# Gate pre-activations of two branches as seven block products ahead of attention, their tanh parked in memory until the merges

## The chip, the cores and the metric

One core of a Trainium2 chip runs the whole kernel; the other cores do nothing. The metric is the device time of one execution in microseconds (us), lower is better. The engines of the core are TensorE (PE in the profile; its weight loads are PEld), VectorE (DVE), ScalarE (ACT), GpSimd (POOL) and SyncE (SP), which issues nearly all DMA transfers. Each engine works its own instruction stream in order, and semaphores connect the streams.

## What is computed

An encoder of two post-norm layers on 512 tokens of width 1024, in float32. One input projection of 6816 columns feeds three mixers and the gates; the part that matters here:

```python
proj = jnp.einsum('bsd,de->bse', x, w_in[l])
(na_q, na_k, na_v, df_q, df_k, df_v, m_cq, m_ckv, m_kr, gate_pre) = jnp.split(proj, split_points, axis=-1)
na_out = neighbourhood_attention(...)     # branch 0, 8 heads of 64
df_out = diff_attention(...)              # branch 1, 4 heads of 2 x 64
mla_out = latent_attention(...)           # branch 2, 8 heads
gates = jax.nn.sigmoid(gate_pre + b_gate[l]).reshape(b, s, 3, 1024)
merged = sum(gates[:, :, i] * (branch_i @ w_branch[l, i]) for i in range(3))
x = layer_norm(alpha * x + merged @ w_out[l], ln1)
gu = x @ w_ffn_in[l]                      # 2 x 2816 columns
x = layer_norm(alpha * x + (silu(gu[..., :2816]) * gu[..., 2816:]) @ w_ffn_out[l], ln2)
```

The gates need only x, not the attention: 3 x 1024 columns for 512 tokens. The kernel uses sigmoid(z) = (1 + tanh(z/2))/2, with the half taken later.

## The kernel before

Every float32 operand is split into a high part and a low rest (`split`, `wsplit`: ScalarE writes the high part, VectorE subtracts it, which gives the low one), and a product is three matmuls, high by high, high by low and low by high (`mm3`). x stands transposed in `xth` and `xtl` (eight blocks of 128 rows, 512 tokens). Weights come by DMA in blocks of 512 KB into a ring of two tiles `raw`, are split into `whi` and `wlo`, and are used by `gemm_w` (weights stationary) or `gemm_x` (activations stationary). PSUM has two banks each under the names `acc`, `sc`, `pv` and `tr`. SBUF slots are handed out by two queues: H with 8 tiles `f` of 1024 columns, R with 38 tiles `r` of 512.

A layer runs: neighbourhood values (`na_values`), the latent input projection with its norms (`latents`), four pairs of neighbourhood heads (`na_pair`), four pairs of latent heads (`mla_proj`, `mla_pair`), four differential heads (`df_proj`, `df_values`, `df_head`), the output projection, and the feed-forward part. In the feed-forward part nine of eleven column groups are computed by `ffn_fast`, seven products of blocks in place of eight: x is cut into two halves of tokens and two of rows, the weights likewise into four blocks, and sums of blocks (for x by `x_sums`, once per layer, on VectorE) take the place of one product. One product (`product`) is 2 x 4 x 3 matmuls of 256 columns.

A differential head goes over four tiles of 128 tokens: scores (L476, L477), maximum on VectorE (L478), exponentials on ScalarE (L479), the mix of the two softmaxes (L483), four transposes (L486), their split (L221, L222), value products (L491, L492), the norm (L494 to L499 with GpSimd's power in between), and last the transposes of the output (L503).

Gates and merges are laid between the heads by the table PLAN. Its entry after each head names steps: `G20h` computes the gate of branch 2, column group 0 (256 columns) into an H slot, `M20` merges it. `gates` loads 1024 x 256 weights and runs 2 x 8 x 3 matmuls of 512 columns into `acc`, with tanh out of PSUM by ScalarE. Python writes the program in this order, and a scheduler then fixes each engine's stream, taking from what is ready by its own model of the engines; a later step of the program can so stand between two steps of an earlier chain.

Of the kernel before, what the change touches and what calls it, by code (L numbers as in the profile page):

```python
# [9 lines left out]
F32 = mybir.dt.float32  # L10
F32R = mybir.dt.float32r
AF = mybir.ActivationFunctionType
# [4 lines left out]
D = 1024  # L17
# [3 lines left out]
D_FF = 2816  # L21
# [8 lines left out]
C_GATE = 3744  # L30
# [6 lines left out]
    "G20h",  # L37
# [8 lines left out]
    "",  # L46
# [35 lines left out]
def trunk(ctx, tc, x, ln_in, w_in, feat, bias, lamv, w_mla, w_mlr, w_mlv, w_branch, w_out,  # L82
          ln1, w_ffn_in, w_ffn_out, ln2, cst, out):
    nc = tc.nc
    V, A, G, T = nc.vector, nc.scalar, nc.gpsimd, nc.tensor
# [11 lines left out]
    R = Slots(cp, NR, 512, F32R, "r")  # L97
# [8 lines left out]
    xd = [xs.tile([128, D], F32, name=f"xd{t}") for t in range(NT)]  # L106

# [11 lines left out]
    def ptile():  # L119
        return dp.tile([128, 512], F32, tag="P", name="P", bufs=4)  # L120
# [388 lines left out]
    def latents(l, g):  # L509
        lat = [H.get() for _ in range(NT)]  # L510
        krs = [i[:, 672:800] for i in lat]
        for i in krs:
            G.memset(i, 0.0)
        for hf in range(2):
            c0 = C_LAT + hf * 336
            src = lambda a, b: [w_in[l, a:b, c0:c0 + 336]]
            ch = wload_ks(src, 336, (3, 3, 2))
            for t in range(NT):
                p = bank("acc")[:, :336]
                gemm_x(p, ch, slice(0, 336), XT, tsl(t), KD)  # L520
                A.activation(lat[t][:, hf * 336:(hf + 1) * 336], p, AF.Copy)
        for t in range(NT):
# [264 lines left out]
    def hidden(gate, up):  # L787

        sg = ptile()
        A.activation(sg, gate, AF.Silu)  # L790
        V.tensor_mul(sg, sg, up)
        hl = (R.get(), R.get())
        split(*hl, sg)
        return hl
# [28 lines left out]
    def ffn_fast(l, m, sums):  # L823


        def load(t, base, kh):
            c = slice(base + m * 128, base + (m + 2) * 128)
            nc.sync.dma_start(t.rearrange("p (k c) -> p k c", k=4),
                              w_ffn_in[l, kh * 512:(kh + 1) * 512, c].rearrange("(k p) c -> p k c", p=128))
            return t  # L830
# [4 lines left out]
        g0, u0, u1 = load(H.get(), 0, 0), load(H.get(), D_FF, 0), load(H.get(), D_FF, 1)  # L835
        s = H.get()
        g1 = load(wp.tile([128, 1024], F32, tag="raw", name="raw", bufs=2), 0, 1)
# [4 lines left out]
        t1, t2, t3, t4 = sums  # L842
# [20 lines left out]
        res = [hidden(px, p1)]  # L863
        res.append(hidden(u2, u3))
        return res
# [24 lines left out]
    for l in range(DEPTH):  # L890
# [19 lines left out]
        tiles, cq, ckv, kr = latents(l, fp[:, 25:30])  # L910
# [3 lines left out]
        def fill(steps):  # L914

            for kind, b, mp, *place in steps:
                b, mp, place = int(b), int(mp), "".join(place)
                if kind == "G":
# [12 lines left out]
                    gates(l, b, mp, bg, gt)  # L931
# [165 lines left out]
```

## Time and profile before

| | |
|---|---|
| median of 3 runs | 1848.38 us (1847.4 to 1851.75) |
| the profiled execution | 1850.09 us |
| its span, first to last instruction | 1847.0 us |
| granted TensorE clock, mean | 0.998 |
| matmuls | 11248 |
| DMA | 195.86 MB, mean 106 GB/s |

The profile is of one execution. A row of the timeline gives start, length, engine, line, operation and what it writes and reads, with the shape; lengths of matmuls overlap, since the next starts before the last has ended. Two thirds of the time are outside the feed-forward part: in layer 0 the neighbourhood heads begin at 92 us, the differential heads at 312 us and the output projection at about 512 us; layer 1 starts at about 900 us.

### The profile page before, as it was taken

To read this page: it belongs to the slowest core of one execution; us is meant where nothing else is said; L and a number is where in the kernel's file an instruction comes from. 1 tells how busy PE (TensorE), PEld (TensorE's weight loads), DVE (VectorE), ACT (ScalarE), POOL (GpSimd) and SP (SyncE) were. 2 spreads that over 40 slices of the span, in tenths; PEclk is the share of its full clock that TensorE was granted. 3 is DMA by queue.
4 is the path that set the end of the run, shared out by engine and by line. 5 is a ranking of instruction groups with operands and counts; after the bars stand their busy time and mean duration, and the time that the engine had idled before them with its cause. 6 is when DMAs were issued, how large, how long until landed. Compare 5 with 4: busy or idle time off the path is not lost.

```text
span 1847.0 us, 28601 instructions
## 1 busy us (share of the span) xinstructions
PE 1814.9 (98%) x11248; PEld 1617.9 (88%) x11248; DVE 1309.9 (71%) x2204; ACT 897.8 (49%) x1612; POOL 90.1 (5%) x165
## 2 busy tenths in 40 slices
PE   7999999999999999999999999999999999999997
PEld 5988899988888999999789888999888799899996
DVE  6488887665568767777756888867655687676766
ACT  4567776555433433334336677755554234333331
POOL 4100000000001000000001000000000000000001
PEclk9999999999999999999999999999999999999999
DMA  7453232222262132323445332322233512323222
GB/s 258 116 164 95 89 94 75 83 78 86 85 201 81 58 114 81 117 89 103 151 123 170 112 98 87 92 63 87 75 98 103 182 58 94 113 92 108 93 98 80
DMA packets 167766, 195.86 MB, mean 106 GB/s; under 512 B 8529, under 2 KB 132689, under 8 KB 167633
## 3 DMA queue, kind: packets, MB, share of 16 engines
q1 hardware_dynamic: 167632, 194.05, 33.7%
q8 instruction: 88, 1.44, 0.3%
q14 instruction: 46, 0.37, 0.1%
HBM read 177.24 MB, written 9.44 MB: 101 GB/s over the span
## 4 chain that ended last, share of the span: by engine, by line
PE 89%; DVE 5%; DMA 3%; ACT 1%; issue 1%; SPq 0%; POOLq 0%; DVEq 0%; POOL 0%; ACTq 0%
PE acc L157 18%; PE acc L158 18%; PE acc L156 17%; PE sc L784 9%; PE pv L784 7%; DVE wlo L139 2%; PE tr L648 2%; PE sc L156 1%; DMA f<-in_w_ffn_in_dram 1%; PE sc L158 1%; PE sc L157 1%; PE pv L157 1%; PE pv L158 1%; PE pv L156 1%; PE pv L491 1%
## 5 line engine op out<-in xcount | busy, mean ns | idle before, releaser
L138 ACT ACTIVATE whi<-raw 128x1024 fp32r<-128x1024 f32 (+3 forms) x246 | 254.3, 1034 | 289.4 <-PE acc L157 54.1
L139 DVE TENSOR_TENSOR wlo<-raw,whi 128x1024 fp32r<-128x1024 f32 (+3 forms) x246 | 293.6, 1195 | 132.2 <-ACT whi L138 129.0
L156 PE MATMUL acc<-xth,whi 128*128 128x512 f32 x512 | 204.0, 399 | 0.3 <-ACT f L672 0.3
L158 PE MATMUL acc<-xth,wlo 128*128 128x512 f32 x512 | 202.7, 396 | 0.0
L157 PE MATMUL acc<-xtl,whi 128*128 128x512 f32 x512 | 202.6, 396 | 0.0
L138 ACT ACTIVATE whi<-f 128x1024 fp32r<-128x1024 f32 x90 | 94.6, 1057 | 182.4 <-PE acc L158 102.3
L157 PE MATMUL acc<-wlo,r 128*128 128x512 f32 (+1 forms) x440 | 171.3, 390 | 2.2 <-DVE wlo L139 2.2
L158 PE MATMUL acc<-whi,r 128*128 128x512 f32 (+1 forms) x440 | 170.7, 389 | 0.0
L156 PE MATMUL acc<-whi,r 128*128 128x512 f32 (+1 forms) x440 | 169.0, 390 | 0.6 <-ACT whi L138 0.5
L157 PE MATMUL acc<-wlo,xth 128*128 128x256 f32 (+2 forms) x544 | 162.4, 299 | 1.3 <-DVE wlo L139 1.3
L156 PE MATMUL acc<-whi,xth 128*128 128x256 f32 (+2 forms) x544 | 161.7, 299 | 1.7 <-ACT whi L138 1.6
L158 PE MATMUL acc<-whi,xtl 128*128 128x256 f32 (+2 forms) x544 | 162.2, 299 | 0.0
L784 PE MATMUL pv<-r,whi 128*128 128x256 f32 x864 | 156.0, 280 | 2.3 <-DVE P L853 2.0
L784 PEld LDWEIGHTS pv<-r,whi 128*128 128x128 f32 x864 | 132.3, 188 | 5.2 <-issue 2.8
L139 DVE TENSOR_TENSOR wlo<-f,whi 128x1024 fp32r<-128x1024 f32 x90 | 109.4, 1221 | 34.7 <-ACT whi L138 34.7
L784 PE MATMUL sc<-xth,whi 128*128 128x256 f32 x432 | 120.5, 279 | 0.0
L784 PE MATMUL pv<-r,wlo 128*128 128x256 f32 x432 | 120.5, 279 | 0.0
L784 PE MATMUL sc<-xtl,whi 128*128 128x256 f32 x432 | 120.3, 279 | 0.0
L784 PE MATMUL sc<-xth,wlo 128*128 128x256 f32 x432 | 119.9, 279 | 0.0
L156 PEld LDWEIGHTS acc<-xth,whi 128*128 128x128 f32 x512 | 96.3, 188 | 19.5 <-ACT f L672 0.7
L157 PEld LDWEIGHTS acc<-xtl,whi 128*128 128x128 f32 x512 | 96.4, 188 | 18.8
L158 PEld LDWEIGHTS acc<-xth,wlo 128*128 128x128 f32 x512 | 96.4, 188 | 18.7
(255 smaller groups left out, 4462.2 us busy)
## 6 DMA issues: line engine op xcount, KB each, us to landing
raw<-in_w_in_dram SPq DMA_DIRECT2D x64, 512.0 KB, 3.7
f<-in_w_ffn_in_dram SPq DMA_DIRECT2D x54, 512.0 KB, 3.7
raw<-in_w_ffn_out_dram SPq DMA_DIRECT2D x44, 512.0 KB, 3.7
raw<-in_w_ffn_in_dram SPq DMA_DIRECT2D x34, 512.0 KB, 3.5
raw<-in_w_in_dram SPq DMA_DIRECT2D x64, 256.0 KB, 3.3
raw<-in_w_branch_dram SPq DMA_DIRECT2D x24, 512.0 KB, 3.3
raw<-in_w_out_dram SPq DMA_DIRECT2D x16, 512.0 KB, 3.6
r<-r SPq DMA_DIRECT2D x56, 128.0 KB, 2.7
```

The costliest lines, as they stand in the source:

```text
L138: A.activation(hi[:, :n], raw[:, :n], AF.Copy)
L139: V.tensor_sub(lo[:, :n], raw[:, :n], f32(hi[:, :n]))
L156: T.matmul(o, lh[0], rh[0], start=first, stop=False)
L157: T.matmul(o, lh[0], rh[1], start=False, stop=False)
L158: T.matmul(o, lh[1], rh[0], start=False, stop=last)
L491: T.matmul(po[:, 0:256], ch_[:, tsl(k)], v, start=k == 0, stop=False)
L648: T.transpose(pt[:, tsl(i)], prs[i % 2][:, tsl(kp + i // 2)], ident)
L784: T.matmul(o[:, c], w[a][:, j, f], x[e], start=fresh and mi == 0 and j == 0 and n == 0, stop=j == 3 and n == 2, skip_group_check=True)
```

## The change

Gates of branches 1 and 2 are computed ahead of attention. `ffn_fast` is cut into `block_set`, which does the seven products for any weights, and the rest. `gates_fast` uses it on two neighbouring column groups at once (256 columns each, as the upper and lower block), applies tanh, and stores the result in a tensor `gd` in the chip's main memory (HBM), one per branch and group. Four sets per layer are laid around the two halves of the latent input projection; `x_sums` is computed for them as well, and given back afterwards. `G` steps of branches 1 and 2 in PLAN then only load the stored tanh into their slot. Branch 0 keeps `gates`. `G20h` moves from the first entry of PLAN (behind the first neighbourhood pair) to the tenth (behind the second of the four differential heads, which are counted from 0 here).

```diff
 PLAN = [i.split() for i in (
-    "G20h",
+    "",
...
     "G03h M03",
-    "",
+    "G20h",
     "M20 G21g G22h M21 M22",
...
+    gd = {(b, mp): xs.tile([128, 1024], F32, name=f"gd{b}{mp}") for b in (1, 2) for mp in range(4)}
...
-    def latents(l, g):
+    def latent_rows(l, between):
         lat = [H.get() for _ in range(NT)]
...
+        between(0)
         for hf in range(2):
             c0 = C_LAT + hf * 336
...
+            between(1 + hf)
+        between(3)
+        return lat
...
-    def ffn_fast(l, m, sums):
+    def block_set(wsrc, top, bottom, sums):
...
-        res = [hidden(px, p1)]
-        res.append(hidden(u2, u3))
-        return res
+        return (px, p1), (u2, u3)
+
+    def ffn_fast(l, m, sums):
+        return [hidden(*i) for i in block_set(w_ffn_in[l], m * 128, D_FF + m * 128, sums)]
+
+    def gates_fast(l, b, mp, bg, sums):
+
+        col = C_GATE + b * D + mp * 256
+        for th, blocks in enumerate(block_set(w_in[l], col, col + 256, sums)):
+            for i, blk in enumerate(blocks):
+                t = ptile() if th == 0 and i == 0 else blk
+                for mi in range(2):
+                    m = b * 8 + 2 * (mp + i) + mi
+                    c = slice(mi * 256, mi * 256 + 256)
+                    A.activation(t[:, c], blk[:, c], AF.Tanh, bias=bg[:, m:m + 1], scale=0.5)
+                dst = gd[b, mp + i].rearrange("p (m t) -> p m t", m=2)
+                nc.sync.dma_start(dst[:, :, th * 256:th * 256 + 256], t.rearrange("p (m t) -> p m t", m=2))
...
-        tiles, cq, ckv, kr = latents(l, fp[:, 25:30])
+        sums = x_sums()
+        lat = latent_rows(l, lambda i: gates_fast(l, 2 - i // 2, i % 2 * 2, bg, sums))
+        for t in sums:
+            for hl in t:
+                R.put(*hl)
+        tiles, cq, ckv, kr = latents(l, fp[:, 25:30], lat)
...
                     if b:
                         held[b, mp] = pool, slot, gt
-                    gates(l, b, mp, bg, gt)
+                        for i in range(2):
+                            nc.sync.dma_start(gt[i], gd[b, mp][:, i * 512:(i + 1) * 512])
+                    else:
+                        gates(l, b, mp, bg, gt)
```

The scheduler's streams move with it. Lines behind the insertion are one or seven higher in the changed kernel (L503 is L504 there, L784 is L791).

The first place is TensorE's stream in layer 0, where the last differential head's keys are transposed (L462, L463 after), ahead of that head's first scores (L476, L477 after). Numbers behind a name are those of the tile: `tr_4632` and `tr_5414` are the transposed keys, `acc_4895` and `acc_4921` gate pre-activations, `acc_5653` and `acc_5670` the first merge of branch 1. Before:

```order
L462 MATMUL tr_4632<-cons_120,f2_114 128x128 x4
L157 MATMUL acc_4895<-xtl_73,whi_4891 128x512
L158 MATMUL acc_4895<-xth_72,wlo_4892 128x512
L156 MATMUL acc_4895<-xth_72,whi_4891 128x512
L157 MATMUL acc_4895<-xtl_73,whi_4891 128x512
L158 MATMUL acc_4895<-xth_72,wlo_4892 128x512
L156 MATMUL acc_4921<-xth_72,whi_4885 128x512
L157 MATMUL acc_4921<-xtl_73,whi_4885 128x512
```

After:

```order
L504 MATMUL tr_5169<-cons_120,ost_5012 128x128 x2
L463 MATMUL tr_5414<-cons_120,f0_112 128x128 x4
L157 MATMUL acc_5653<-r18_92,whi_5649 128x512
L157 MATMUL acc_5670<-r18_92,whi_5649 128x512
L158 MATMUL acc_5653<-r19_93,whi_5649 128x512
L159 MATMUL acc_5653<-r18_92,wlo_5650 128x512
L158 MATMUL acc_5670<-r19_93,whi_5649 128x512
L159 MATMUL acc_5670<-r18_92,wlo_5650 128x512
L477 MATMUL sc_5438<-r24_98,r14_88 128x512
L477 MATMUL sc_5443<-r8_82,r15_89 128x512
```

Before, 24 matmuls of gates stand between the transposes and the first scores; after, six of a merge.

The second place is the same head a little later, between the scores of its second tile of tokens and the next scores (before), and over its second and third tile (after). `acc_4995` is a gate. Before:

```order
L476 MATMUL sc_4695<-r24_98,r26_100 128x512
L477 MATMUL sc_4695<-r25_99,r26_100 128x512
L156 MATMUL acc_4995<-xth_72,whi_4985 128x512
L157 MATMUL acc_4995<-xtl_73,whi_4985 128x512
L158 MATMUL acc_4995<-xth_72,wlo_4986 128x512
L156 MATMUL acc_4995<-xth_72,whi_4985 128x512
```

After:

```order
L478 MATMUL sc_5482<-r9_83,r15_89 128x512
L477 MATMUL sc_5516<-r24_98,r14_88 128x512
L478 MATMUL sc_5516<-r25_99,r14_88 128x512
L487 MATMUL tr_5451<-cons_120,P_5436 128x128 x4
L477 MATMUL sc_5521<-r8_82,r15_89 128x512
L478 MATMUL sc_5521<-r9_83,r15_89 128x512
L477 MATMUL sc_5555<-r24_98,r14_88 128x512
L478 MATMUL sc_5555<-r25_99,r14_88 128x512
L487 MATMUL tr_5490<-cons_120,P_5475 128x128 x4
```

Before, fourteen gate matmuls follow these scores; after, the head's own steps stand one behind the other, and so from its first scores to its last transposes. Head 2 of each layer reads the same.

The third place is VectorE's stream at the end of the neighbourhood values in layer 0. `xtl` is the low part of x, `r<-acc` halves of values. Before:

```order
L222 TENSOR_TENSOR xtl<-tr,xth 128x4x128
L222 TENSOR_TENSOR r_78<-acc,r_78 128x2x128
L222 TENSOR_TENSOR r_79<-acc,r_79 128x2x128
L139 TENSOR_TENSOR wlo<-raw,whi 128x1008 x2
L222 TENSOR_TENSOR r_80<-acc,r_80 128x2x128
```

After:

```order
L223 TENSOR_TENSOR xtl<-tr,xth 128x4x128
L764 TENSOR_TENSOR gt<-xth,gt 128x512
L223 TENSOR_TENSOR r_91<-gt,r_90 128x512
L765 TENSOR_TENSOR gt<-gt,xtl 128x512
L223 TENSOR_TENSOR r_78<-acc,r_78 128x2x128
L768 TENSOR_TENSOR xs<-gt,xth 128x512
L771 TENSOR_TENSOR gt<-xth,gt 128x512
L223 TENSOR_TENSOR r_89<-gt,r_88 128x512
L852 TENSOR_TENSOR f_117<-f_115,f_116 128x1024
```

The sums of x (L761 to L772, with their splits) and the first set's weights (L852 to L854) now stand between the last low part of x and the latent projection's weights.

More of the change, by code (lines that the diff above doesn't have):

```diff
@@ L506, in df_head @@
         return o
-    def latents(l, g):
+    def latent_rows(l, between):
         lat = [H.get() for _ in range(NT)]
-        krs = [i[:, 672:800] for i in lat]
-        for i in krs:
-            G.memset(i, 0.0)
+        between(0)
         for hf in range(2):
@@ L521, in latents @@
                 A.activation(lat[t][:, hf * 336:(hf + 1) * 336], p, AF.Copy)
+            between(1 + hf)
+        between(3)
+        return lat
+    def latents(l, g, lat):
+        krs = [i[:, 672:800] for i in lat]
+        for i in krs:
+            G.memset(i, 0.0)
         for t in range(NT):
@@ L821, in ffn_plain, with load @@
         return res
-    def ffn_fast(l, m, sums):
-        def load(t, base, kh):
-            c = slice(base + m * 128, base + (m + 2) * 128)
+    def block_set(wsrc, top, bottom, sums):
+        t1, t2, t3, t4 = sums
+        def load(t, col, kh):
             nc.sync.dma_start(t.rearrange("p (k c) -> p k c", k=4),
-                              w_ffn_in[l, kh * 512:(kh + 1) * 512, c].rearrange("(k p) c -> p k c", p=128))
+                              wsrc[kh * 512:(kh + 1) * 512, col:col + 256].rearrange("(k p) c -> p k c", p=128))
             return t
@@ L833, in halved @@
             return wsplit(t, 1024)
-        g0, u0, u1 = load(H.get(), 0, 0), load(H.get(), D_FF, 0), load(H.get(), D_FF, 1)
+        g0, u0, u1 = load(H.get(), top, 0), load(H.get(), bottom, 0), load(H.get(), bottom, 1)
         s = H.get()
-        g1 = load(wp.tile([128, 1024], F32, tag="raw", name="raw", bufs=2), 0, 1)
+        g1 = load(wp.tile([128, 1024], F32, tag="raw", name="raw", bufs=2), top, 1)
         px, py, pz = bank("sc"), bank("pv"), bank("sc")
@@ L841, in ffn_fast @@
         A.activation(p1, px, AF.Copy)
-        t1, t2, t3, t4 = sums
         with tc.high_priority():
```

## The prediction

> **What bounds the kernel now.** I read the busy shares of the page first, then the stretches of layer 0, then single chains in the timeline. The first row below is the page's; the others are a view of stretches (us; instructions in brackets): neighbourhood heads, latent heads, then the four differential heads one by one.
>
> ```profile
> PE 1814.9 (98%) x11248; PEld 1617.9 (88%) x11248; DVE 1309.9 (71%) x2204; ACT 897.8 (49%) x1612; POOL 90.1 (5%) x165
> ...
> core 0: us, PE busy (x) PEld busy (x) DVE busy (x) ACT busy (x) POOL busy (x), PEclk, DMA share, GB/s
> ...
> 100.00:180.00 80.00, 79.70 (x441) 68.55 (x440) 68.72 (x205) 56.89 (x138) 0.00 (x0) 1.00 0.37 112
> 180.00:312.00 132.00, 132.00 (x836) 118.00 (x835) 105.09 (x202) 94.69 (x190) 0.00 (x0) 1.00 0.29 87
> ...
> 410.00:460.00 50.00, 50.00 (x298) 43.80 (x297) 30.78 (x54) 26.55 (x54) 3.65 (x8) 1.00 0.29 85
> 460.00:505.00 45.00, 45.00 (x225) 37.57 (x224) 22.96 (x42) 21.82 (x44) 3.62 (x8) 1.00 0.25 83
> ```
>
> TensorE is busy for the whole of attention, while VectorE is at 80 to 86% in the first two stretches and at 50 to 60% in the last two differential heads. So TensorE's issue sets the time, and it does so because the in-order stream always has a matmul that waits for nothing between two steps of a softmax chain. The gates' matmuls are much of that filler. The time therefore follows from two things: how many matmul slots the change removes, and whether the stream still has filler where a chain is waiting.
>
> **The matmuls.** TensorE starts the next matmul before the last one ends, so I price a matmul by the distance of starts, not by its duration. The first row is from the chain that ended last (start, length, count), the others are two 512-column matmuls 23 starts apart, and a weight load group of the products.
>
> ```profile
> 639.87 5.65 PE sc L784 x48
> ...
> 1305.19 0.39 PE L156 MATMUL acc<-xth,whi 128*128 128x512 f32 x1
> 1310.45 0.39 PE L158 MATMUL acc<-xth,wlo 128*128 128x512 f32 x1
> ...
> L784 PEld LDWEIGHTS sc<-xth,whi 128*128 128x128 f32 x432 | 81.0, 188 | 0.9
> ```
>
> A 256-column matmul costs 5.65/48 = 0.1177 us, a 512-column one 5.26/23 = 0.2287 us. Per layer eight gates go, each with 2 x 8 x 3 = 48 matmuls of 512 columns; four sets come, each with 7 products x 2 x 4 x 3 = 168 matmuls of 256. Over two layers: 768 x 0.2287 = 175.6 us go and 1344 x 0.1177 = 158.2 us come, a gain of 17.4 us. It is not 1/8, because two half-width matmuls cost 0.235 against 0.229.
>
> One rule speaks against this term. The Trainium skill ("TensorE: Matmul & The Clock Gate", The mechanism, of its part on packing small matmuls) says that a weight load overlaps a matmul in flight only when it goes to another row group. All loads here fill the whole array, so by that rule load and matmul would follow each other, and with the 188 ns of the row the change would cost 1344 x 0.306 - 768 x 0.417 = 91 us instead of gaining. The trace disagrees: starts 118 ns apart with loads of 188 ns between them are only possible when they overlap, and the feed-forward part runs this very form today. I keep the 17.4 and give the rule no chance.
>
> **VectorE and ScalarE in the sets.** A set splits seven 1024-wide halves and adds four more 1024-wide ones where two gates split four, and it adds five 512-wide additions. The sums of x add 26 operations of 512 per layer.
>
> ```profile
> 598.28 0.69 DVE L754 TENSOR_TENSOR gt<-xth 128x512 f32<-128x512 f32 x1
> 600.09 0.69 DVE L755 TENSOR_TENSOR xs<-xtl 128x512 f32<-128x512 f32 x1
> ...
> 335.56 1.22 DVE L139 TENSOR_TENSOR wlo<-raw,whi 128x1024 fp32r<-128x1024 f32 x1
> 336.69 0.34 DVE L495 SCALAR_TENSOR_TENSOR ost<-pv,ring,otmp 128x128 f32<-128x128 f32 x1
> ```
>
> Three starts in 1.81 us give 0.603 us for 512 columns; 1.13 us for 1024. Per layer VectorE gets 4 x (7 x 1.13 + 5 x 0.603) = 43.7 plus 15.7 us, in all some 119 us over the kernel (1310 to about 1429). A set is then 11 x 1.13 + 5 x 0.603 = 15.4 us of VectorE under 168 x 0.1177 = 19.8 us of TensorE, as in the feed-forward part: hidden, as long as the sums are there in time.
>
> They are not. The sums need all of x transposed, and the third product of the first set reads the last of them. These rows are the last low half of x and the first matmul after the neighbourhood values, in layer 0 and in layer 1.
>
> ```profile
> 34.44 0.69 DVE L222 TENSOR_TENSOR xtl<-tr,xth 128x512 fp32r<-128x512 f32 x1 [2.59 <-ACT xth L221]
> 41.55 0.32 PE L156 MATMUL acc<-whi,xth 128*128 128x336 f32 x1
> ...
> 946.99 0.69 DVE L222 TENSOR_TENSOR xtl<-tr,xth 128x512 fp32r<-128x512 f32 x1 [2.52 <-ACT xth L221]
> 953.92 0.32 PE L156 MATMUL acc<-whi,xth 128*128 128x336 f32 x1
> ```
>
> In the new order VectorE has, between that low half and the sum that the third product needs, 9 operations of 1024, 22 of 512 and 4 of 256 (taken at 0.34): 24.8 us, so the sum is ready at 59.9. TensorE has 102 matmuls of the set before it reaches that point: 41.55 + 12.0 = 53.5. A wait of 6.4 us. In layer 1 the same count gives 972.6 against 966.2, again 6.4. Together 12.8 us. Nothing stands behind the waiting products in TensorE's queue that could go first. Bounds: 5 us if the sums start earlier than I read, 20 if ScalarE's halves come late as well.
>
> **The differential heads.** This is the large term. In the new order heads 0 and 1 keep their filler (the next head's projections, merges of branch 2). Heads 2 and 3 have none: projections and merges are used up, and the gates that stood there are gone. The two accumulator banks hold the first product of branch 1's merge, which needs head 3, so nothing else may start. TensorE then goes at the pace of the chain. The rows give that chain: scores, maximum and exponentials to the mix, the tempo of two tiles, the transposes and the split, and, from the last value product on, the norm up to the next transpose.
>
> ```profile
> 332.46 0.40 PE L477 MATMUL sc<-r,r 128*128 128x512 f32 x1
> 325.95 0.74 DVE L483 SCALAR_TENSOR_TENSOR P<-P,ring 128x512 f32<-128x512 f32 x1
> 331.61 0.74 DVE L483 SCALAR_TENSOR_TENSOR P<-P,ring 128x512 f32<-128x512 f32 x1
> 334.89 0.75 DVE L483 SCALAR_TENSOR_TENSOR P<-P,ring 128x512 f32<-128x512 f32 x1
> 338.13 0.60 PE L486 MATMUL tr<-cons,P 128*128 128x128 f32 x4
> 338.77 0.60 ACT L221 ACTIVATE PP<-tr 128x512 fp32r<-128x512 f32 x1 [0.23 <-PE tr L486]
> 336.95 0.68 DVE L222 TENSOR_TENSOR PP<-tr,PP 128x512 fp32r<-128x512 f32 x1
> ...
> 495.68 0.22 PE L492 MATMUL pv<-r,PP 128*128 128x128 f32 x1
> 495.74 0.29 PE L503 MATMUL tr<-cons,ost 128*128 128x128 f32 x1
> 495.94 0.37 ACT L494 ACTIVATE otmp<-pv,ring 128x128 f32<-128x128 f32 x1 [3.14 <-PE pv L492]
> 497.52 0.57 POOL L232 TENSOR_TENSOR ring<-ring,expo 128x1 f32<-128x1 f32 x1
> 498.12 0.29 DVE L499 TENSOR_SCALAR ost<-ost,ring 128x128 f32<-128x128 f32 x1 [1.43 <-POOL ring L232]
> ```
>
> Scores to the end of the mix: 335.64 - 332.46 = 3.2 us. Tempo: 334.89 - 331.61 = 3.3 us per tile, the shortest of the trace. Mix to the last transpose: 0.1 + 0.64 + 0.60 + 0.68 + 0.6 (rest of the value matmuls) + 2.9 (495.68 to 498.6) = 5.5 us. A head of four tiles that nothing covers lasts 3.2 + 3 x 3.3 + 5.5 = 18.6 us. In it TensorE has only 12 score matmuls, 16 transposes (0.06 each, from the starts 495.68 and 495.74), 16 value pairs and the norm's transposes: 7.0 us in head 2, 6.8 in head 3. Waits: 11.6 and 11.8 us. Ahead of head 3 its keys must be split and copied by DMA, and behind it the output is scaled before the merge goes on:
>
> ```profile
> 399.49 0.38 PE L462 MATMUL tr<-cons,f 128*128 128x128 f32 x2
> 402.06 0.47 SPq L297 DMA_DIRECT2D r<-r  x1
> r<-r SPq DMA_DIRECT2D x56, 128.0 KB, 2.7
> 503.06 0.69 ACT L224 ACTIVATE r<-tr,fp 128x512 fp32r<-128x512 f32 x1 [1.57 <-PE tr L503]
> 503.78 0.75 DVE L225 SCALAR_TENSOR_TENSOR r<-tr,fp,r 128x512 fp32r<-128x512 f32 x1 [1.03 <-ACT r L224]
> ```
>
> From the transposes to a landed copy 2.6 + 2.7 = 5.3 us, for the second half-head 1.2 later; with the last score 6.7 us, under which TensorE has 2.5 us (six merge matmuls and four scores): 4.2 us of wait. Behind: 0.3 + 1.5 = 1.8 us. Sum per layer 11.6 + 4.2 + 11.8 + 1.8 = 29.4, in two layers 58.8 us. Bounds, since no uncovered head stands in the trace: VectorE's own work in the two heads and between them (15 maxima, 8 mixes, 8 splits, norms and key halves, 32 us by the durations of their groups) against TensorE's 16.3 leaves 16 us per layer, 32 in all; with the 5.7 us a tile of a covered head (325.95 to 331.61) it would be 87. I take 3.3, because without filler a tile waits only for its own chain. Layer 1 has the same order as layer 0.
>
> **What costs nothing.** Weights: the same bytes as before. The stored tanh is 16 stores and 16 loads of 256 KB per layer, 16.8 MB in all beside 196 MB, with the DMA engines at 25 to 37% in the stretches above; loads stand in SP's queue ahead of weight loads and wait for a free slot as the gates did; if that cover goes, the merge waits one landing, about 3 us, inside a head that waits 11 anyway. ScalarE, at 49%, gets three more conversions of about 1 us per set. The neighbourhood heads lose one gate (11 us of filler) per layer. By the new order VectorE has 185 us of work from the last low half of x (35.1) to the first latent head, so it could be there at 220; TensorE has 204 us of slots from 41.55 and the wait of 6.4, 252. With 30 us of slack I take 0; the bound is what (c) gives.
>
> **Sum.** 1850.1 us for the profiled execution (span 1847.0) - 17.4 + 12.8 + 58.8 = 1904.3. The median of the runs is 1.7 us lower: **1903 us**.
>
> **Rivals.**
> (a) The clock drops as well. At the kernel's start, after idle time, 512-column matmuls stand 0.42 us apart, twice the later 0.23:
>
> ```profile
> 15.10 0.63 PE L158 MATMUL acc<-whi,xtl 128*128 128x512 f32 x1
> 15.52 0.63 PE L156 MATMUL acc<-whi,xth 128*128 128x512 f32 x1
> ```
>
> Heads that leave TensorE idle for two thirds of 18 us could bring that back: about 1.5 us more in first scores and last products of each of four heads and 2 us of slow matmuls behind each layer's pair, 10 us: 1913. Against it: no single wait in a head is longer than about 3 us. The Trainium skill (same page, What's actually happening) says that an idle window of about 3.4 us halves the clock; by that rule only the wait for the key copies comes near.
> (b) The heads run at VectorE's own work: 32 instead of 58.8, 1876 us. For it: buffers for two tiles. Against it: 3.3 is the best tempo seen.
> (c) VectorE becomes the bound from the sets to the latent heads, where it is already at 86%: if its 30 us of slack are lost to waiting for loads, about 10 us per layer, 1923.
> (d) The other side: the heads' waits are covered after all and only the removed slots count, 1831 to 1844. It decides where a bare head takes under 8 us, a tile under 1 us; VectorE's two maxima and one mix alone are 2 us per tile. Or gain and waits cancel, 1843 to 1854.
>
> **How the numbers follow.** My forecast 0.67 (1885 to 1922), (a) 0.10, (b) 0.10, (c) 0.05, (d) faster 0.05, cancelled 0.03. A change under 0.3% (5.5 us) can't be told from none here. Slower 0.92, same 0.03, faster 0.05. The range runs from (b) with the shorter wait for the sums, rounded down, 1866, to (c) with some of (a), 1930.
>
> **What would show it.** TensorE busy well under 98%, with gaps in two stretches per layer just before the output projection; the mixes of heads 2 and 3 about 3.3 us apart where TensorE's groups say it waited for the probabilities; waits for the sums' halves in the first set; 256-column products still 0.118 apart; VectorE near 1430 us. If the mixes stand under 2 us apart, or TensorE shows no gaps in heads 2 and 3, the large term is wrong and with it the sign.

## The result and the profile after

| | before | after |
|---|---|---|
| median of the runs | 1848.7 us (1847.4 to 1851.8) | 1938.2 us (1931.0 to 1939.0) |
| ratio of the times | 1 | 1.047, 95% interval 1.0445 to 1.0501 |
| profiled execution, span | 1850.1 us, 1847.0 us | 1931.0 us, 1929.0 us |
| TensorE matmuls, busy | 11248, 98% | 11824, 95% |
| VectorE busy | 1309.9 us | 1427.3 us |
| mean granted clock | 0.998 | 0.976 |

The change made the kernel 4.7% slower. I had forecast 1903 us, at most 1930: the direction was right, the size was not. All executions here and below ran at about one speed except one: an execution of experiment e4 took 3284 us at a granted clock of 0.726, where its other three took 1948 to 1949, and its ratio leaves it out. Lines of the changed kernel stand one higher than before below L507 (the mix is L484) and seven higher behind the new function (the products are L791).

The page of the changed kernel answers the first rows of the prediction: busy shares, and the granted clock in 40 slices.

```profile
PE 1839.7 (95%) x11824; PEld 1651.7 (86%) x11824; DVE 1427.3 (74%) x2352; ACT 937.5 (49%) x1692; POOL 87.2 (5%) x165
...
PEclk9999999999889999999999999999997999999999
```

TensorE fell from 98 to 95%, VectorE came to 1427.3 us where the count of its operations gave 1429, and the clock has dips, in the slices from 482 to 579 us and from 1447 to 1495. The view of stretches of layer 0 shows where: the first set, the later sets, the start of the neighbourhood heads, latent heads and differential heads 0 and 1, and last heads 2 and 3.

```profile
core 0: us, PE busy (x) PEld busy (x) DVE busy (x) ACT busy (x) POOL busy (x), PEclk, DMA share, GB/s
...
36.00:60.00 24.00, 15.40 (x66) 12.62 (x64) 18.84 (x26) 9.57 (x15) 0.00 (x0) 0.79 0.46 117
60.00:160.00 100.00, 99.58 (x787) 98.73 (x787) 69.82 (x90) 47.58 (x69) 0.00 (x0) 1.00 0.48 141
160.00:190.00 30.00, 25.53 (x150) 21.94 (x149) 17.68 (x34) 19.29 (x46) 8.88 (x16) 0.94 0.55 150
...
320.00:498.00 178.00, 178.00 (x1224) 163.77 (x1223) 129.91 (x234) 109.55 (x223) 6.81 (x16) 1.00 0.33 98
498.00:556.00 58.00, 42.69 (x172) 29.87 (x171) 37.95 (x82) 27.76 (x74) 6.63 (x16) 0.74 0.11 34
```

Three stretches have idle TensorE and a lowered clock; between them TensorE is as full as before. To compare with the forecast I give each stretch an **excess**: the distance of the first and last matmul start in it, less its matmuls at their paces (0.2287 us for 512 columns, 0.1177 for 256, 0.153 for 336, 0.06 for 128). It contains waits and slow matmuls alike.

| stretch, layer 0 / layer 1 | excess before | excess after | grew by | forecast |
|---|---|---|---|---|
| first set or latent product to the latents' transposes | 1.4 / 0.3 | 13.6 / 12.2 | 24.1 | 12.8 |
| neighbourhood heads up to the first latent query's transposes | 2.2 / 1.8 | 9.4 / 8.5 | 13.9 | 0 |
| on to head 2's first score | 15.6 / 16.4 | 16.1 / 15.4 | -0.5 | 0 |
| heads 2 and 3, and 6 us behind | 4.3 / 4.3 | 36.3 / 35.7 | 63.4 | 58.8 |
| the rest | 33.6 | 31.9 | -1.7 | 0 |
| matmuls at their paces | 1748.3 | 1730.9 | -17.4 | -17.4 |

Together 81.8 us, where the spans differ by 82.0. The last row is counts times paces, so it had to meet its forecast; what the run can show is whether the pace held, and it did: 48 products of a gate set on the chain that ended last take the 5.65 us of the feed-forward part before.

```profile
142.03 5.65 PE sc L791 x48
```

The heads' term is right to 5 us; the first two stretches hold 25 of the 27 us by which the profiled execution (1931.0) exceeds the sum of the prediction (1904.3). The other 7 us up to the median lie between executions of this kernel: the profiled one was the shortest of the four.

The bare heads first. The mixes of head 2, the score product that waits for head 3's copied keys, and the last norm transposes of heads 2 and 3, in the timeline of the changed kernel:

```profile
502.08 0.75 DVE L484 SCALAR_TENSOR_TENSOR P<-P,ring 128x512 f32<-128x512 f32 x1
504.73 0.75 DVE L484 SCALAR_TENSOR_TENSOR P<-P,ring 128x512 f32<-128x512 f32 x1
508.56 0.74 DVE L484 SCALAR_TENSOR_TENSOR P<-P,ring 128x512 f32<-128x512 f32 x1
512.30 0.73 DVE L484 SCALAR_TENSOR_TENSOR P<-P,ring 128x512 f32<-128x512 f32 x1
521.00 0.47 PE L504 MATMUL tr<-cons,ost 128*128 128x128 f32 x1 [1.71 <-DVE ost L500]
523.86 0.63 PE L158 MATMUL acc<-r,whi 128*128 128x512 f32 x1
524.29 0.63 PE L159 MATMUL acc<-r,wlo 128*128 128x512 f32 x1
529.44 0.50 PE L478 MATMUL sc<-r,r 128*128 128x512 f32 x1 [1.48 <-DMA r<-r]
548.88 0.47 PE L504 MATMUL tr<-cons,ost 128*128 128x128 f32 x1 [1.87 <-DVE ost L500]
```

The mixes stand 2.7, 3.8 and 3.7 us apart, 3.4 on the mean, where I had taken 3.3. From the end of the last mix to the last transpose it is 8.0 us where I had put 5.5. Two stretches of head 2, from its first mix to the end of its last and from there to its last transpose, show that these two parts have different limits:

```profile
502.08:513.03 10.95, 7.71 (x43) 5.48 (x42) 10.58 (x26) 6.52 (x21) 1.58 (x4) 0.99 0.07 27
513.03:521.10 8.07, 5.75 (x25) 4.66 (x24) 2.76 (x8) 2.94 (x9) 1.58 (x4) 0.50 0.00 0
```

Between the mixes VectorE is busy for 10.58 of 10.95 us and the clock is whole, so VectorE's queue sets the tempo there. In the tail VectorE is idle for two thirds, no engine is full, and the clock is at half. The two merge products between the heads start 0.43 us apart: half pace.

The first sets, in both layers. The first two rows are VectorE's block sum of weights and the product behind it, in layer 0; then two products at half pace; the last is the wait for a sum of x in layer 1.

```profile
43.95 1.23 DVE L852 TENSOR_TENSOR f<-f,f 128x1024 f32<-128x1024 f32 x1 [4.71 <-DMA f<-in_w_in_dram]
47.58 0.58 PE L791 MATMUL sc<-xth,wlo 128*128 128x256 f32 x1 [4.86 <-DVE wlo L140]
47.95 0.41 PE L791 MATMUL sc<-xth,whi 128*128 128x256 f32 x1
48.17 0.41 PE L791 MATMUL sc<-xtl,whi 128*128 128x256 f32 x1
...
1012.99 1.31 PE L791 MATMUL sc<-r,whi 128*128 128x256 f32 x2 [4.62 <-ACT r L222]
```

Layer 1 waits for the sum as forecast (4.6 us against 6.4), but the wait is followed by some 4 us of products 0.21 us apart instead of 0.1177, and so is that in layer 0. In layer 0 the wait is another one: VectorE stands 4.7 us in its queue until weights land, and TensorE for VectorE. From there on VectorE has no room left:

```profile
43.95:66.00 22.05, 14.93 (x87) 13.78 (x88) 21.50 (x29) 8.94 (x14) 0.00 (x0) 0.77 0.34 92
```

In layer 1 it is as full around the wait, 19.93 of 20 us from 997 to 1017.

At the first neighbourhood head a latent norm waits for GpSimd, ScalarE for VectorE, and the first scores for ScalarE:

```profile
175.18 0.35 DVE L535 TENSOR_SCALAR f<-f,ring 128x256 f32<-128x256 f32 x1 [1.05 <-POOL ring L233]
176.28 0.59 ACT L306 ACTIVATE r<-acc 64x512 fp32r<-64x512 f32 x1 [2.21 <-DVE r L307]
180.17 0.50 PE L379 MATMUL sc<-r,r 128*128 128x256 f32 x2 [2.98 <-ACT r L318]
182.90 0.41 PE L157 MATMUL acc<-whi,r 128*128 128x256 f32 x1
183.12 0.41 PE L158 MATMUL acc<-wlo,r 128*128 128x256 f32 x1
```

### The profile page after: what moved, and what is told of

The parts are those of the page before. It is cut to its first block, busy times and chain, and to the rows that moved or that the text cites. A ratio compares the mean times of both kernels' runs of the same rounds, so it can differ in the third digit from the quotient of the medians.

```text
span 1929.0 us, 30163 instructions
## 1 busy us (share of the span) xinstructions
PE 1839.7 (95%) x11824; PEld 1651.7 (86%) x11824; DVE 1427.3 (74%) x2352; ACT 937.5 (49%) x1692; POOL 87.2 (5%) x165
## 4 chain that ended last, share of the span: by engine, by line
PE 81%; DVE 8%; DMA 4%; ACT 3%; issue 2%; POOL 1%; SPq 0%; DVEq 0%; POOLq 0%; ACTq 0%
PE acc L157 13%; PE acc L158 13%; PE acc L159 13%; PE sc L791 13%; PE pv L791 10%; DVE wlo L140 2%; PE tr L655 1%; PE pv L158 1%; PE sc L157 1%; PE pv L159 1%; PE sc L159 1%; PE sc L158 1%; PE pv L157 1%; DMA f<-in_w_in_dram 1%; ACT whi L139 1%
## 5 line engine op out<-in xcount | busy, mean ns | idle before, releaser
L139 ACT ACTIVATE whi<-raw 128x1024 fp32r<-128x1024 f32 (+5 forms) x230 | 237.0, 1032 | 278.5 <-DVE raw L865 56.6
L140 DVE TENSOR_TENSOR wlo<-raw,whi 128x1024 fp32r<-128x1024 f32 (+5 forms) x230 | 273.9, 1193 | 69.5 <-ACT whi L139 67.5
L791 PE MATMUL pv<-r,whi 128*128 128x256 f32 x1248 | 224.9, 280 | 6.0 <-DVE P L861 2.3
L791 PEld LDWEIGHTS pv<-r,whi 128*128 128x128 f32 x1248 | 191.1, 188 | 9.7 <-ACT whi L139 2.9
L791 PE MATMUL sc<-xth,wlo 128*128 128x256 f32 x624 | 174.4, 280 | 6.2 <-DVE wlo L140 6.1
L791 PE MATMUL sc<-xth,whi 128*128 128x256 f32 x624 | 175.2, 281 | 0.6 <-ACT whi L139 0.6
L791 PE MATMUL sc<-xtl,whi 128*128 128x256 f32 x624 | 174.4, 280 | 0.0
L791 PE MATMUL pv<-r,wlo 128*128 128x256 f32 x624 | 174.0, 279 | 0.0
L791 PEld LDWEIGHTS sc<-xth,wlo 128*128 128x128 f32 x624 | 117.9, 189 | 7.4 <-DVE wlo L140 6.8
L791 PEld LDWEIGHTS sc<-xth,whi 128*128 128x128 f32 x624 | 118.2, 189 | 2.4 <-ACT whi L139 1.4
L791 PEld LDWEIGHTS sc<-xtl,whi 128*128 128x128 f32 x624 | 118.0, 189 | 1.5
L791 PEld LDWEIGHTS pv<-r,wlo 128*128 128x128 f32 x624 | 117.5, 188 | 0.0
L157 PEld LDWEIGHTS acc<-whi,xth 128*128 128x128 f32 x544 | 102.4, 189 | 5.6 <-ACT whi L139 3.3
L158 PEld LDWEIGHTS acc<-wlo,xth 128*128 128x128 f32 x544 | 102.8, 189 | 4.7 <-DVE wlo L140 2.4
```

The lines of the kernel that those rows point to most:

```text
L139: A.activation(hi[:, :n], raw[:, :n], AF.Copy)
L140: V.tensor_sub(lo[:, :n], raw[:, :n], f32(hi[:, :n]))
L157: T.matmul(o, lh[0], rh[0], start=first, stop=False)
L158: T.matmul(o, lh[0], rh[1], start=False, stop=False)
L791: T.matmul(o[:, c], w[a][:, j, f], x[e], start=fresh and mi == 0 and j == 0 and n == 0, stop=j == 3 and n == 2, skip_group_check=True)
```

## The experiments

All times are medians; the kernel before ran at 1847 to 1850 us beside each of them. None was faster than it.

### Is it the place or the product form (e1, e2, e3)

e1 and e2 keep one branch as block products and compute the other as before; e2 also puts `G20h` back into the first entry of PLAN:

```
-  lambda i: gates_fast(l, 2 - i // 2, i % 2 * 2, bg, sums)
+  lambda i: gates_fast(l, 2, i * 2, bg, sums) if i < 2 else None     # e1; e2: branch 1
...
   if b:
       held[b, mp] = pool, slot, gt
+  if b == 2:                                                         # e1; e2: b == 1
       ...                                                            # load the stored tanh
   else:
       gates(l, b, mp, bg, gt)
```

> Only branch 2's gates come as block products ahead of attention; branch 1's four gates stand as plain ones where they stood before. In the changed kernel the trace has TensorE's excess over its matmul slots in four places: the first set (about 10 us in layer 0, 12 in layer 1), the start of the first neighbourhood head (7 and 6), and differential heads 2 and 3 with what follows (34 and 34), against the kernel before. Theory U (heads 2 and 3 cost because nothing fills them): 44 us of gates per layer are back, more than the 34 missing, so the heads' 68 us go. With half the gain of slots (8.7), the first sets' 22 and the neighbourhood start's 13: 1848.7 - 8.7 + 22 + 13 = 1875 us. Rival (the heads are slow for another reason, such as the stored tanh's transfers): 1938 + 8.7 = 1947 us.

> The mirror image: only branch 1's gates come as block products ahead; branch 2's four are plain, the first of them behind the first neighbourhood head as before. Heads 2 and 3 then have three plain gates and four merges, 55 us per layer, as filler. Theory U: enough, the heads' 68 us go as well. Theory N (the first neighbourhood head starts late because the gate that filled it is gone): those 13 us go too, and 1848.7 - 8.7 + 22 = 1862 us come out, 13 us under the run with branch 2 alone. Rival to N (the sets load VectorE and the queues, so the latents' norms come late): the 13 us stay, 1875 us. Rival to U (only branch 1's gates can fill heads 2 and 3): 1862 + 68 = 1930 us.

e3 keeps the place and the stored tanh, and computes eight plain products:

```
+  def gates_early(l, b, mp0, bg):
+      for mp in (mp0, mp0 + 1):
+          t = (ptile(), ptile())
+          gates(l, b, mp, bg, t)
+          for mi in range(2):
+              nc.sync.dma_start(gd[b, mp][:, mi * 512:(mi + 1) * 512], t[mi])
```

> The place without the product form: both branches' gates are computed ahead of attention, where the sets stand, but each by its eight plain products; their tanh is stored and loaded at the merges as in the changed kernel. No sums of x, no block sums. Theory: the cost is the place. The heads' 68 us and the neighbourhood start's 13 stay, the first sets' 22 go, the 17.4 us of saved slots go as well: 1848.7 + 68 + 13 = 1930 us. Rival (the product form's VectorE work makes the neighbourhood start late): 1848.7 + 68 = 1917 us. Rival (the product form is what costs in the heads too): near 1850 us.

Measured: e1 1909.0 us (ratio 1.0325, 1.0309 to 1.034), e2 1897.4 (1.0266, 1.0249 to 1.0283), e3 1931.1 (1.0446, 1.0429 to 1.0463).

e3 came out at its theory's 1930: without any block product nearly the whole loss is there, so most of it is the place's. The form adds the first sets' waits (24.1 us) and saves the slots (17.4), which is near the 7 us between e3 and the changed kernel. e3's excess grew by 65 us in and behind heads 2 and 3, and by 9.5 at the first neighbourhood heads. e1 and e2 differ by 11.6 us, near the 13 that the missing gate at the first neighbourhood head should cost; e2's excess there is that of before (2.1 us). The match is partly luck: over both layers e1's excess is only 7 us above e2's there, and another 11 on the way to head 2.

But both are 34 to 35 us above what was expected: the heads' loss did not go, it about halved (29 and 28 us of excess where the changed kernel has 63.4). The stretches of e2's differential head 2 and head 3 show how:

```profile
456.00:499.00 43.00, 43.00 (x265) 38.06 (x264) 30.03 (x54) 22.02 (x48) 3.65 (x8) 1.00 0.35 104
504.50:526.00 21.50, 14.48 (x78) 10.15 (x76) 15.21 (x34) 10.85 (x32) 3.70 (x8) 1.00 0.18 56
```

Head 2 is full, head 3 is bare. The filler that was left seems to have gone to the first chain that had a wait, and head 3 found none.

### Is it the clock (e4, e5)

Both add matmuls to heads 2 and 3 that do no work, most of them into a part of the value bank that nothing reads. e4 has 64 per head: those shown and eight between the scores and transposes of each of the last two tiles. e5 has 40: fewer in both places (four for eight there), and twelve ahead of the first scores, into the score banks.

```
+  for k in range(24 if t == 3 else 8):        # e5: 8 if t == 3 else 4
+      T.matmul(po[:, 256:512], cl_[:, tsl(k % NT)], vals[k % NT][:, 0:256], start=True, stop=True)
```

> The changed kernel with 64 added matmuls of 256 columns in each of differential heads 2 and 3, into a part of the value bank that nothing reads: they do no work and fill waits. Nothing else changes. In the changed kernel these heads show matmuls at half the usual pace (512 columns every 0.43 us) for some 32 us of layer 0. Theory C (the lost clock costs on top of the chain): with TensorE kept busier the pace comes back to 0.23, last value products, key transposes and first scores shorten, about 7 to 10 us per layer, 1938 - 14 to 20 = 1918 to 1924 us. Rival (the chain of VectorE, ScalarE and the key copies sets the heads' length, and slow matmuls lie in its waits): 1936 to 1942 us at a higher clock.

> As e4, with fewer idle matmuls and none that the chain has to pass: in each of heads 2 and 3 twelve of 256 columns ahead of the first scores, eight between scores and transposes, four behind each tile's value products and eight behind the last (e4 had 24 there, 2.9 us that stood ahead of the key transposes and of the norm's). In e4 the fourth mix to the last value product took 4.7 us at full pace against 5.6 in the changed kernel. Theory C (the lost clock costs on top of the chain): 1 to 2 us per head and 1 to 2 us behind it come back, 1928 to 1934 us. Rival (slow matmuls lie in waits that the chain sets): 1936 to 1942 us.

Measured: e4 1949.0 us (1.0541, 1.0523 to 1.0558), e5 1939.4 (1.0485, 1.0469 to 1.05). In e4 the 24 matmuls behind the last tile lay on the chain and made it longer: from the start of head 2's last mix to its last transpose it took 10.5 us instead of 8.7. e5 is the better test. Stretches of heads 2 and 3 of layer 0, first the changed kernel, then e5, with the tail of its head 2 in between:

```profile
493.20:521.10 27.90, 21.21 (x97) 15.80 (x96) 20.59 (x44) 13.18 (x37) 3.15 (x8) 0.85 0.25 80
...
525.60:549.00 23.40, 16.55 (x69) 11.05 (x67) 15.15 (x33) 11.69 (x34) 3.48 (x8) 0.72 0.05 12
```

```profile
497.50:525.80 28.30, 24.00 (x138) 19.24 (x136) 21.64 (x46) 13.97 (x38) 3.27 (x8) 1.00 0.27 79
...
518.20:525.80 7.60, 5.51 (x42) 4.77 (x41) 3.24 (x9) 3.10 (x9) 2.35 (x6) 1.00 0.01 2
...
529.00:554.50 25.50, 18.55 (x97) 13.75 (x96) 15.47 (x34) 11.90 (x34) 3.50 (x8) 0.87 0.07 20
```

With the clock at 1.00 instead of 0.85 head 2 takes 28.3 us instead of 27.9. The whole head is a rough measure, since the twelve matmuls ahead of its scores made its start longer and the changed kernel's clock was whole up to the last mix. The tail tells more: from the start of the last mix to the last transpose it took 8.7 us at half clock and 8.3 at the whole one (8.4 and 8.3 in layer 1). So e5 won back 0.2 to 0.4 us; the rest of the tail is the chain's, unless the eight idle matmuls behind the last tile hide a little more. For head 3 the test is weaker: its clock only came to 0.87, and the added matmuls took room of their own. The lost clock is a consequence in head 2 more than a cost on top; for head 3 that is not shown.

### Is it the first set's waits (e6)

```
-  lambda i: gates_fast(l, 2 - i // 2, i % 2 * 2, bg, sums)                    # sets at 0 1 2 3
+  lambda i: [gates_fast(l, 2 - k // 2, k % 2 * 2, bg, sums) for k in ((), (0,), (1,), (2, 3))[i]]
```

> The changed kernel with its four sets put later among the latent rows: the first set behind the first half of the latent columns, the second behind the second half, then the other two; before, the first stood ahead of both halves. The same instructions. Theory F (the first set's waits, 10 us in layer 0 and 12 in layer 1, are for the sums of x and its first weights, and 14.6 us of other matmuls ahead cover them): 1938 - 22 = 1916 us. With the latents done 20 us earlier their norms can run under the last two sets; if the late start of the first neighbourhood head (13 us) comes from late norms, that goes too, 1903 us. Rival (VectorE cannot keep up with the sets, wherever they stand): 1934 to 1938 us.

Measured: 1915.9 us (1.0356, 1.0341 to 1.0372), the 1916 of theory F. The layer 1 stretch with the sets now has TensorE full:

```profile
960.00:1100.00 140.00, 139.41 (x1020) 133.24 (x1019) 111.83 (x156) 65.49 (x100) 4.04 (x8) 1.00 0.50 146
```

Between the two profiled executions the gain is 14 us, since that of the changed kernel was 7 us under its median; in layer 0 a wait of 5.7 us that ends at 47.7 stays. The neighbourhood heads did not gain (excess 9.9 and 10.5). This does not clear the late norms as a cause, since the latent norms came no earlier for it: the last of them starts 3.4 us ahead of the first scores in e6 (170.3 and 173.7) as in the changed kernel (176.8 and 180.2).

### Does it matter where the filler stands (e7, e8)

e7 puts a plain gate of branch 0 behind the first neighbourhood head instead of the fourth (`G00h` in the first row of PLAN). e8 holds branch 2's merges back until head 1 is done (names shortened):

```
+  V.scalar_tensor_tensor(o2[:, 0:1], head1[:, 0:1], 0.0, o2[:, 0:1], op0=OP.mult, op1=OP.add)
...
   qk = df_proj(l, h)
+  if h == 3: fill(PLAN[10])          # branch 2's merges, written behind head 2 before
```

> The changed kernel with one plain gate of branch 0 (11 us of TensorE per layer) put behind the first neighbourhood head instead of the fourth. e2, which had a plain gate there, was 11.6 us under e1, which had none. Theory N (that head waits for want of a filler): its waits of 7 and 6 us go, 1925 us. Rival (the gate is missed as much where it stood, among the latent heads): 1936 to 1940 us.

> The changed kernel with branch 2's merges (22 us of TensorE per layer) held back until differential head 1 is done: one addition of zero times a column of head 1's output makes their first operand depend on it, and they are written behind the projections of head 3. In the changed kernel's trace those merges and projections are all used up in heads 0 and 1. By the new order head 1 has the projections of head 3 as filler, head 2 the merges, head 3 nothing. Theory U (a head without filler costs some 17 us more than it has matmuls for, and the filler was spent early, not missing): only head 3 stays bare, 1938 - 34 = 1904 us. Rival (heads 0 and 1 go bare instead): 1930 to 1940 us.

Measured: e7 1951.3 us (1.0548, 1.0532 to 1.0564), e8 1932.7 (1.045, 1.0432 to 1.0467). Both theories named the right wait and missed the price; e8 came out in the range of its rival, e7 above its own. Stretches of e7: the neighbourhood start, where the gate came to, and the latent heads that lost it, with two waits of the latter from its timeline.

```profile
160.00:190.00 30.00, 29.11 (x167) 24.84 (x166) 17.87 (x26) 19.53 (x41) 8.01 (x16) 1.00 0.52 146
...
240.00:285.00 45.00, 38.11 (x197) 30.88 (x195) 37.14 (x122) 31.38 (x81) 0.00 (x0) 0.96 0.31 94
```

```profile
251.57 0.45 PE L396 MATMUL tr<-cons,P 128*128 128x128 f32 x1 [1.71 <-DVE P L392]
...
283.18 0.50 PE L638 MATMUL sc<-r,r 128*128 128x512 f32 x1 [1.50 <-ACT P L644]
```

The neighbourhood start is full and at full clock: the excess there fell from 9.4 and 8.5 to 3.7 and 2.3 us. On the way to head 2 it rose from 16.1 and 15.4 to 27.9 and 28.4. Twelve us saved, 24 lost. In e8 likewise (between heads 1 and 2, then head 2 and head 3):

```profile
480.00:488.40 8.40, 7.84 (x24) 6.18 (x25) 3.98 (x7) 3.02 (x5) 0.00 (x0) 0.63 0.36 102
488.40:523.00 34.60, 31.42 (x161) 25.74 (x159) 28.64 (x56) 16.25 (x38) 3.41 (x8) 1.00 0.38 122
...
527.00:551.00 24.00, 16.78 (x69) 11.67 (x67) 15.15 (x33) 11.79 (x35) 3.49 (x8) 0.78 0.05 12
```

Head 2 is filled now. The excess of heads 2 and 3 fell by 14 us over both layers, that ahead of them, from the latent heads to head 2, rose by 15. The profiled executions of e8 and of the changed kernel differ by 2 us; the 5 us between the medians are within the changed kernel's own spread. Filler that is moved moves the wait.

### How much filler costs how much (e9, e10)

e9 is e2 with e6's place; e10 has one set per layer, for branch 1's gates 2 and 3.

```
+  lambda i: gates_fast(l, 1, (i - 1) * 2, bg, sums) if i in (1, 2) else None   # e9
+  lambda i: gates_fast(l, 1, 2, bg, sums) if i == 2 else None                   # e10
```

> e2 (branch 1 alone as block products, branch 2 plain) with e6's place: the first set behind the first half of the latent columns, the second behind the second half. Theory: the terms add. e2 was 1897 us, the first set's waits are 22 us: 1875 us, of which the plain kernel's 1848.7 less 8.7 us of slots, and some 35 us of waits in and behind head 3 of the two layers, the only head that e2 leaves bare. Rival (the sets' waits and head 3's share a cause, so that one saving takes the other's place): 1885 to 1897 us.

> Half of e9: per layer one set alone, for branch 1's third and fourth gate, behind both halves of the latent columns; six gates per layer stay plain in their places. 22 us of filler per layer leave attention instead of 44 (e9) and 88 (the changed kernel). Theory L (a share of filler taken is a share of wait, from the first one on): 1848.7 - 4.4 + about 13 to 17, 1857 to 1862 us. Rival (there was slack: with 22 us less every head still finds filler): only the saved slots count, 1844 to 1846 us, which would beat the kernel before by 0.2%.

Measured: e9 1876.4 us (1.0148, 1.013 to 1.0167), 1.4 above its sum. The terms add, but the close number is partly luck: the heads cost 28 us, not 35, and a wait of 6.8 us in layer 0 that ends at 48.2 makes up for it. e10 1869.9 (1.0116, 1.01 to 1.0131), above both of its theories. The excess of heads 2 and 3 and the 6 us behind them grew, over before, per layer by 7 us in e10 (22 us of gates taken from attention), 14 in e9 (44 us) and 32 in the changed kernel (88 us): about a third of every us taken, from the first one on. There was no slack, and that part of theory L holds. Most of what e10 has beyond its sum is in front, in layer 0: a wait of 6.5 us that I had counted to the sums of x. Its timeline:

```profile
44.08 1.23 DVE L852 TENSOR_TENSOR f<-f,f 128x1024 f32<-128x1024 f32 x1 [5.16 <-DMA f<-in_w_in_dram]
...
48.02 0.65 PE L157 MATMUL acc<-whi,xth 128*128 128x336 f32 x1 [6.46 <-DVE r L223]
```

### The late load in layer 0 (e11, e12)

```
-  V.tensor_add(s, u0, u1)
+  (G if late else V).tensor_add(s, u0, u1)      # late: the gate sets
```

> e10 with one instruction of each gate set moved from VectorE to GpSimd: the sum of the two lower weight blocks. In e10's layer 0 VectorE stood 5.2 us at 38.9 to 44.1 in that sum, waiting for its weights to land, with the split of the neighbourhood values behind it in the queue; TensorE waited 6.5 us for that split at 41.5. Layer 1 has no such wait. Theory Q (a high-priority instruction at the head of VectorE's queue waits for a load that I priced at nothing): 1870 - 6 = 1864 us, and the wait at 41.5 is under 1 us. Rival (VectorE is simply late there because of the sums of x): the wait stays, 1868 to 1871 us.

> The same move in the changed kernel with all four sets. There VectorE stood 4.7 us in layer 0 in the same sum (39.2 to 43.95) and TensorE 4.9 us at 42.6 for the low half of the first weights, later in both layers for the sums of x. Theory Q: layer 0 loses that first wait, 1938 - 5 = 1933 us; what is left of the first set's waits is for the sums of x, near the 6.4 us per layer that I forecast. Rival (the sums are behind by so much that the wait only moves): 1936 to 1939 us.

Measured: e11 1872.4 us (1.0138, 1.0121 to 1.0154), e12 1932.8 (1.046, 1.0441 to 1.0479). e11 refutes the cure: the wait moved. Its timeline and its stretch of 30 to 40 us:

```profile
44.22 2.35 POOL L852 TENSOR_TENSOR f<-f,f 128x1024 f32<-128x1024 f32 x1 [14.12 <-DMA f<-in_w_in_dram]
...
46.34 0.77 ACT L139 ACTIVATE whi<-raw 128x672 fp32r<-128x672 f32 x1 [4.19 <-DMA raw<-in_w_in_dram]
...
46.61 1.23 DVE L853 TENSOR_TENSOR f<-f,f 128x1024 f32<-128x1024 f32 x1 [3.14 <-POOL f L852]
...
47.16 0.42 PE L157 MATMUL acc<-whi,xth 128*128 128x336 f32 x1 [2.13 <-ACT whi L139]
```

```profile
30.00:40.00 10.00, 10.00 (x47) 8.10 (x47) 9.09 (x17) 5.41 (x11) 0.10 (x1) 1.00 0.99 314
```

VectorE now stands 3.1 us in the next operation, behind GpSimd, and TensorE waits for the latent weights instead, which land late as well. From 30 to 40 us the DMA engines are at 99%. That alone is not the cause, for in the kernel before they stand at 98% in the same stretch, and TensorE is full. The first row is from the kernel before, the second from the changed kernel's chain that ended last:

```profile
30.00:40.00 10.00, 10.00 (x46) 8.08 (x46) 4.38 (x8) 4.38 (x8) 0.08 (x1) 1.00 0.98 286
...
38.12 5.71 DMA f<-in_w_in_dram
```

What is new is a load among them that VectorE needs at once. The last of the first set's three blocks, which that sum needs, is issued only at 38.12, behind other transfers in SyncE's stream, and takes 5.7 us to land, where the 24 loads of its kind take 4.3 on the median. How the late issue and the slow landing share the wait was not separated. e12 met its number, but within the changed kernel's spread (1931 to 1939), and a wait of 5.7 us followed at 52.0 there; it decides nothing. How layer 0's 13.6 us divide between late loads and late sums stays open.

## Why the prediction was right and wrong

- **The direction**, and its reason: right. Heads 0 and 1 kept their filler (excess 1.7 and 2.0 us in layer 0, as before) and head 3 had none. Head 2 had some at its start, against what the prediction says and the section on the change ("Head 2 of each layer reads the same"): 24 merge products stand between its first scores, from 493.5 to 499.4 us. The tiles came 3.4 us apart against 3.3 forecast, but for another reason in part: I took the tempo of a tile that waits only for its own chain, and between head 2's mixes VectorE's queue was full. The heads' term was 58.8 and measured 63.4. That is closer than its parts: 8.6 us of waits stood there before already, so the waits after are 72 us; what was short is above all the tail, 5.5 us a head against 8.0 and 7.1 in layer 0, where transposes, splits and the norm wait for each other on ScalarE, VectorE and GpSimd.
- **The matmuls**: right as far as the trace can tell: 768 of 512 columns went, 1344 of 256 came, and these still start 0.1177 us apart under weight loads of 188 ns. The rule of the Trainium skill on row groups ("TensorE: Matmul & The Clock Gate", The mechanism), which would have cost 91 us, does not agree with the trace after either; the same section also lets a load for the background weight buffer go ahead, and that would fit.
- **"The neighbourhood heads lose one gate ... I take 0"**: the step that failed most. It measured 13.9 us. I had compared VectorE's work with TensorE's over 200 us and found 30 us of slack; but the wait is a chain of short steps at one place, and such a sum doesn't show it. e7 took most of the wait away with a gate, and e2, which kept the gate, never had it. The missing gate is not the whole of it: e1 and e12, without it too, have 5.7 and 5.3, and 4.8 and 6.2 us of excess there where the changed kernel has 9.4 and 8.5. What makes up the difference stays open, late norms among the candidates.
- **"Weights: the same bytes as before ... costs 0"**: failed in layer 0. The bytes are the same, but a block that VectorE needs at once is issued at 38.12 us and lands 5.7 us later, and VectorE stands still for 4.7. With it the **first sets** were mis-sized: 24.1 us, not 12.8. The wait for the sums in layer 1 was smaller than forecast (4.6 us against 6.4); what came on top are the load in layer 0, shorter waits for VectorE and ScalarE, and the products at half pace behind them, all of which the sum had at nothing. With VectorE full at that time, the half pace may have cost nothing of its own. e6 took 14 us (profiled executions) to 22 us (medians) away by putting 14.6 us of other matmuls ahead.
- **Rival (a), the clock**: its sign was right, its place wrong. The clock did fall, to 0.85 and 0.72 in heads 2 and 3, and my argument against it (no single wait over 3 us) was no argument: it fell there behind waits under 1.9 us. But in head 2 keeping it up won 0.2 to 0.4 us (e5). Whether half pace adds to the time elsewhere, behind the waits of the first sets, at the neighbourhood start and in the first merge products behind head 3, was not measured by itself.
- **Rivals (b), (c), (d)**: their times were not seen, the reasons of (b) and (c) in part. VectorE is 65% busy over heads 2 and 3 (37.95 of 58 us), but that is an average: between the mixes of head 2 it is full (10.58 of 10.95), as (b) has it, and in the tails it is not. (c) has VectorE as the bound from the sets to the latent heads: it is full in the first sets (21.50 of 22.05 us in layer 0, behind a wait for a load), and not behind them (69.82 of 100 us from 60 to 160). For (d) no wait was covered.
- **The range**: its top held part of (a) and (c) as alternatives. What happened was the forecast, with the neighbourhood start that I had priced at nothing and the first sets at twice their price; another 7 us lie between the profiled execution and the median.

## What to carry to other kernels

Where an in-order engine is full because independent work fills the waits of a chain, that work has a price as filler: here a gate moved out of attention freed its slots and gave about a third of them back as waits in two heads, besides the waits where it went. Moving other filler into the gap moves the wait (e7, e8), and keeping the clock up with idle matmuls won 0.2 to 0.4 us in a head whose length the chain sets (e5). Read an engine's share over a chain in parts: VectorE, 65% busy over two heads, was full between the mixes and idle in the tails. So price a move chain by chain at both ends, with the loads of that moment, before counting the matmuls that it saves.

## What was not expected of the hardware

The clock fell without a long wait: in heads 2 and 3 no wait that the trace shows exceeded 1.9 us, and still matmuls ran at half pace (0.43 us per 512 columns). The granted clock was 0.62 on the mean from 512.72 to 553.68 us in layer 0. Once lost the full clock stayed lost for 3.4 us or a multiple of it: the granted clock is 0.50 over 953.04 to 956.45 and 181.63 to 185.04 us, 3.41 us each, over 45.09 to 51.90 (6.8 us), 543.44 to 553.68 (10.2) and 512.72 to 526.37 (13.7). The Trainium skill ("TensorE: Matmul & The Clock Gate", What's actually happening) describes a monitor of the array's activity over windows of about 3.4 us; the trace agrees with that length, but not with the condition of a whole idle window. The same page (A second HAM failure mode: psum-queue depth-cycling) tells of short idle times between groups of matmuls that make the clock oscillate, and the two heads look like that.

A 1024-column addition of two f32 tiles took 2.35 us on GpSimd in e11, against 1.23 us on VectorE.
